# Weights loaded and split by whole blocks of 1024 columns, and q and k rotated by full-height products, in a float32 decoder step on one core

## The chip, the cores and the metric

The kernel runs on one core of one Trainium2 chip. The time is the device time of an execution in microseconds (us), and the number that counts is the median of several runs. Each core has a matrix engine (PE, with its weight loads shown apart as PEld), a vector engine (DVE), a scalar engine (ACT), a general engine (POOL) and a queue that starts the transfers (SP).

## The reference

The reference is one inference step of a hybrid decoder of two layers with 1024 features, all in float32. Two groups of requests share the weights: one prompt of 512 tokens and eight sequences of 4 new tokens each, so that 544 tokens go through every projection.

```python
for l in range(2):
    h = rms_norm(x, norm1_w[l])
    qr, kr, vr, gr, qa, ka, va = split(h @ w_in[l])         # 7 x 512 columns
    qr, kr = rotary(4 heads of 128), rotary(4 heads of 128)
    qa, ka = rotary(8 heads of 64), rotary(8 heads of 64)
    y = silu(gr) * group_norm(retention(qr, kr, vr, state_ret))
    o = dilated_attention(qa, ka, va, cache_k, cache_v)     # windows (128,1) (512,4) (2048,16)
    x = x + concat(y, o) @ w_out[l]
    x = x + (silu(g) * val) @ w_down[l]    # g, val: causal conv, width 3, of norm(x) @ w_up[l]
y = rms_norm(x, final_norm_w)

def rotary(x, pos):       # of one head, halves x1 and x2
    return concat([x1 * cos - x2 * sin, x2 * cos + x1 * sin])
```

Besides y it returns the rotated keys and the values of every new token, the retention states and the last rows that the convolution needs.

## The kernel before

**Layout.** Features lie on the partitions and tokens along a row: a tile of one block of 128 features is 128 x 544, and in PSUM two halves of 272 tokens (HC). The matrix engine multiplies in a reduced float32 form (fp32r), and the kernel gets float32 accuracy from three products: each weight and each activation is split into a high and a low part (wh and wl, xh and xl), and a block of 128 output features sums wh·xh, wh·xl and wl·xh over the blocks of the input. With 8 input blocks (nk = 8) that is 8 x 3 x 2 = 48 matmuls of 128 x 272; w_out (nk = 4, two passes of eight blocks) and w_down (nk 5, 5, 4, 4, 4 in five groups of eight blocks) have shorter blocks.

**The main list.** `main` holds all blocks in the order in which PE multiplies them: in each layer 28 blocks of w_in, 16 of w_out, 44 of w_up, 40 of w_down. In w_in the order is va0, va1, ka0, qa0, ka1, qa1, va2, ka2, qa2, va3, ka3, qa3, then vr, kr, qr for each of four heads, then the four gates; each of these blocks holds 128 columns, so a block of ka or qa holds two heads of 64 and a block of kr or qr one head of 128.

**Weights.** `add_block` cuts a block with nk over 4 in two parts of (nk+1)//2, so a w_in block comes in two parts of 512 columns; `halves` numbers the parts of all blocks with s. When PE's code comes to part s, `load_w(s+6)` puts the load of a later part on SP (tag raw, 6 buffers), and `split_w(s+3)` lets ACT copy part s+3 to wh and spawns DVE's subtraction that leaves wl (5 buffers each). PE's code for part s waits for that with `parts_of(s)`.

**Rotation.** Each block of q or k has an evacuation from PSUM (`ka(hp)`, `qa(hp)`, `kr(h)`, `qr(h)`) that calls `rotary_out`: DVE multiplies the whole block by cos (tile ra), and then, for each half of each head in it, the other half by sin (tile rb, pieces of 32 or 64 partitions); POOL adds the two, the 512 prompt tokens and the 32 sample tokens apart.

**What sets the order.** The code of the attention and the retention is written as generators, which `st.spawn` queues. While PE's code of the blocks is written out, `st.pump` and `st.until` step these generators, whenever a model of the engines' clocks (class Clock) says that their inputs are ready. So PE's blocks (tiles ps) are mixed with the attention's and the retention's small matmuls (tiles sec), and the place of each is fixed when the kernel is built. `blk` hands out 51 buffers in turn for all tiles of 128 x 544. Every instruction is recorded by one helper, so that nearly all of the trace's rows have line L112; they are told apart by their tiles.

Of the kernel before, what the change touches and what calls it, by code (L numbers as in the profile page):

```python
# [9 lines left out]
F32 = mybir.dt.float32  # L10
F32R = mybir.dt.float32r
# [6 lines left out]
NT = SEQ + NB * T  # L18
HC = NT // 2
PC = SEQ // 2  # L20
SC = NB * T // 2
KB = D // 128
ZB = 28
FB = 22
GROUPS = ((0, 5), (5, 10), (10, 14), (14, 18), (18, 22))
EPS = 1e-6
# [14 lines left out]
NPAR = 48  # L41
NCONV = 352
EARLY = 640


SEM = {"pe": 0.22, "act": 0.2, "dve": 0.14, "pool": 0.08, "sp": 0.1}
# [179 lines left out]
def trunk(ctx: ExitStack, tc: tile.TileContext, xin, w_in, w_out, w_up, w_down, kc, vc, s0, sctx_d, params_d,  # L226
# [69 lines left out]

    def add_block(src, nk, rhs, evac, pre=None):
        i = len(main)
        parts = [(0, nk)] if nk <= 4 else [(0, (nk + 1) // 2), ((nk + 1) // 2, nk)]
        main.append(dict(src=src, nk=nk, rhs=rhs, evac=evac, pre=pre, first=len(halves), parts=parts))  # L300
        for a, b in parts:
            halves.append((i, a, b))
# [3 lines left out]
    def load_w(s):  # L306
        if s < len(halves):
            i, a, b = halves[s]
            raw[s] = rotate(wpool.tile([128, b - a, 128], F32, name=name("raw"), tag="raw", bufs=6), "raw", 6)
            sp.dma_start(raw[s], main[i]["src"][:, a:b, :])  # L310

    def split_w(s, at_once=False):
        if s < len(halves):
            i, a, b = halves[s]
            if i >= len(main) - KB:
                hi, lo = (blk([128, b - a, 128], F32R, n) for n in ("wh", "wl"))
            else:
                hi, lo = (rotate(wpool.tile([128, b - a, 128], F32R, name=name(n), tag=n, bufs=5), n, 5)
                          for n in ("wh", "wl"))
# [160 lines left out]
    def two(ap, w):  # L480
        return ap.rearrange("p (c n) -> p c n", c=2)
# [2 lines left out]
        dve.tensor_mul(two(dst[:, 0:SEQ], PC), ps[:, :, 0:PC], rstd[:, :, 0:PC])  # L484
        dve.tensor_mul(two(dst[:, SEQ:NT], SC), ps[:, :, PC:HC], rstd[:, :, PC:HC])

    def rotary_out(ps, cos, sin, half, dst):
        a = blk([128, 2, HC], F32, "ra")
        b = blk([128, 2, HC], F32, "rb")
        dve.tensor_mul(a, ps[:, :, :HC], cos)  # L490
        for q in range(0, 128, 2 * half):
            lo, hi = slice(q, q + half), slice(q + half, q + 2 * half)
            dve.tensor_mul(b[lo], ps[hi, :, :HC], sin[hi])
            dve.tensor_mul(b[hi], ps[lo, :, :HC], sin[lo])
        pool.tensor_add(two(dst[:, 0:SEQ], PC), a[:, :, 0:PC], b[:, :, 0:PC])
        pool.tensor_add(two(dst[:, SEQ:NT], SC), a[:, :, PC:HC], b[:, :, PC:HC])

    def rsqrt_small(out, var, n):
        v = small([128, n], "rsv", 2)
# [382 lines left out]
    def mixer(l):  # L882
# [69 lines left out]
                store(kv_o[l, 1, hp], L.va[hp])  # L952
            return evac

        def ka(hp):
            def evac(ps):
                L.ka[hp] = blk([128, NT], F32, "ka")
                rotary_out(ps, *L.tab[2], 32, L.ka[hp])
                pool.tensor_copy(L.ks[:, hp, :], L.ka[hp][:, SEQ:])
                store(kv_o[l, 0, hp], L.ka[hp])  # L960
            return evac

        def qa(hp):
            def evac(ps):
                L.qa[hp] = blk([128, NT], F32, "qa")
                rotary_out(ps, *L.tab[2], 32, L.qa[hp])
                for s in range(2):
                    r = slice(64 * s, 64 * s + 64)
                    c = (2 * hp + s) * T
                    pool.tensor_copy(L.qpad[r, hp, :, c:c + T],  # L970
                                     L.qa[hp][r, SEQ:].rearrange("p (b t) -> p b t", b=NB))
                L.cat[4 + hp] = blk([128, 2, HC], F32, "cat")
                L.have.add(("qa", hp))
                if hp == 2:
                    start_ret()
                if hp == 3:
                    L.tab.pop(2)
                    rope_tables(L, l, 0)()
                    fold_tables(L, 0, norm)
            return evac  # L980

        def g(h):
            def evac(ps):
# [12 lines left out]
                scaled_out(ps, norm.rstd, L.vr[h])  # L996
            return evac

        def kr(h):
            def evac(ps):  # L1000
                L.kr[h] = blk([128, NT], F32, "kr")
                rotary_out(ps, *L.tab[0], 64, L.kr[h])
            return evac

        def qr(h):
            def evac(ps):
                L.qr[h] = blk([128, NT], F32, "qr")
                rotary_out(ps, *L.tab[0], 64, L.qr[h])
                L.cat[h] = blk([128, 2, HC], F32, "catr")
                L.have.add(("qr", h))  # L1010
                if h == 3:
                    L.tab.pop(0)
            return evac

        rhs = rhs_of(norm)
        order = [(24, va(0)), (25, va(1))]
        for hp in range(4):
            order += [(24 + hp, va(hp))] * (hp > 1) + [(20 + hp, ka(hp)), (16 + hp, qa(hp))]
        for h in range(4):
            order += [(8 + h, vr(h)), (4 + h, kr(h)), (h, qr(h))]  # L1020
        for h in range(4):
            order.append((12 + h, g(h)))
        for n, (zb, evac) in enumerate(order):
# [156 lines left out]
        else:  # L1180
            load_w(n)
    load_w(4)
    load_w(5)
    for what, n in start:
        if what == "x":
            list(first.scale(n))
# [19 lines left out]
    sp.dma_start(cst[0], consts_d[:, :EARLY])  # L1206
    ps = [main_bank() for _ in range(2)]
    for k in range(KB):
        if k == 4:
            load_w(6)  # L1210
            load_w(7)
            split_w(4)
        if k == 6:
            split_w(5)
            split_w(6)
        for n in range(2):
            s = 2 * n + k // 4
            products(main[n], ps[n], k, parts_of(s), k // 4 * 4)
            if k % 4 == 3:
                split.pop(s)  # L1220
            if k == KB - 1:
                main[n]["evac"](ps[n])
                ps[n] = None
            st.pump(0.7)
    load_w(8)
    load_w(9)
    sp.dma_start(cst[1], consts_d[:, EARLY:])
    sp.dma_start(taps, params_d[:, NPAR:])

    for i, b in enumerate(main[2:-KB]):  # L1230
        st.block = i + 2
        if b["pre"]:
            b["pre"]()
        ps = main_bank()
        for pi, (a, e) in enumerate(b["parts"]):
            s = b["first"] + pi
            load_w(s + 6)
            split_w(s + 3)
            w = parts_of(s)
            split.pop(s)  # L1240
            for k in range(a, e):
                products(b, ps, k, w, a)
                st.pump(0.7)
        b["evac"](ps)
        st.pump()
# [3 lines left out]
    for c in range(2):  # L1249
        for n, b in enumerate(main[-KB:]):  # L1250
            s, nk = b["first"], b["nk"]
            if c == 0:
                load_w(s + 6)
                split_w(s + 3)
# [14 lines left out]
def _tables():  # L1269
# [51 lines left out]
    for first, half in ((0, 64), (2, 32)):  # L1321
        e = (-np.arange(half, dtype=f) / f(half)).astype(f)
        inv = np.power(10000.0, e.astype(np.float64)).astype(f)
        ang = (p[None, :] * inv[:, None]).astype(f).astype(np.float64)
        cos, sin = _chunk(np.cos(ang).astype(f)), _chunk(np.sin(ang).astype(f))
        rope[:, first] = np.concatenate([cos] * (128 // half))
        rope[:, first + 1] = np.concatenate([sin, -sin] * (64 // half))
    return out, rope


# [6 lines left out]
def _layout(i):  # L1337
    g = {k: np.asarray(v) for k, v in i.items()}
    a = {}
    tok = np.concatenate([g["x_prompt"].reshape(SEQ, D), g["x_sample"].reshape(NB * T, D)])  # L1340
    a["xin"] = _chunk(tok.T.reshape(KB, 128, NT).transpose(1, 0, 2))

    def w(n):
        m = g[n]
# [50 lines left out]
```

## Time and profile before

| | |
|---|---|
| median of 3 runs | 1444.94 us (1444.93 to 1448.46) |
| profiled execution | 1444.82 us |
| its span | 1443.0 us |
| mean granted clock of PE | 0.997 |
| PE busy | 1423.1 us (99%) |
| DVE busy | 949.2 us (66%) |
| ACT busy | 571.6 us (40%) |
| POOL busy | 178.9 us (12%) |

The span is the time from the first to the last instruction of the profiled execution; 1.8 us of its own time lie around it. Busy is the sum of an engine's instructions; matmuls overlap one another, so PE at 99% says that it hardly ever lacked an instruction, and the time of one matmul is read from the spacing of starts.

### The profile page before, as it was taken

To read this page: it belongs to the slowest core of one execution; us is meant where nothing else is said; L and a number is where in the kernel's file an instruction comes from. 1 tells how busy PE (TensorE), PEld (TensorE's weight loads), DVE (VectorE), ACT (ScalarE), POOL (GpSimd) and SP (SyncE) were. 2 spreads that over 40 slices of the span, in tenths; PEclk is the share of its full clock that TensorE was granted. 3 is DMA by queue.
4 is the path that set the end of the run, shared out by engine and by line. 5 is a ranking of instruction groups with operands and counts; after the bars stand their busy time and mean duration, and the time that the engine had idled before them with its cause. 6 is when DMAs were issued, how large, how long until landed. Compare 5 with 4: busy or idle time off the path is not lost.

```text
span 1443.0 us, 29646 instructions
## 1 busy us (share of the span) xinstructions
PE 1423.1 (99%) x11634; PEld 1356.0 (94%) x11634; DVE 949.2 (66%) x1857; ACT 571.6 (40%) x1108; POOL 178.9 (12%) x553
## 2 busy tenths in 40 slices
PE   8999999999999999999999999999999999999997
PEld 8888788999999999999998878899999999999996
DVE  8876556588775565757678765566977647566665
ACT  4454333444443333424435442243444424333334
POOL 4212222000000000000022221120000000000003
PEclk9999999999999999999999999999999999999999
DMA  6315682433222222223322339722422232322231
GB/s 237 97 60 181 233 311 89 154 113 115 93 80 88 91 83 101 93 84 104 104 90 90 119 105 316 283 91 101 148 104 88 65 112 70 107 88 89 88 93 63
DMA packets 98635, 173.92 MB, mean 121 GB/s; under 512 B 11072, under 2 KB 21440, under 8 KB 98496
## 3 DMA queue, kind: packets, MB, share of 16 engines
q1 hardware_dynamic: 98496, 172.03, 35.3%
q8 instruction: 92, 1.51, 0.4%
q14 instruction: 47, 0.39, 0.1%
HBM read 159.77 MB, written 12.21 MB: 119 GB/s over the span
## 4 chain that ended last, share of the span: by engine, by line
PE 94%; DVE 3%; issue 1%; DMA 0%; ACT 0%; SPq 0%; DVEq 0%; POOL 0%; ACTq 0%
PE ps L112 82%; PE sec L112 12%; DVE wl L112 1%; DVE rb L112 1%; DMA x<-xin 0%; DVE p L112 0%; SPq L112 0%; DVE xl L112 0%; DVE ra L112 0%; DVE sq L112 0%; ACT xh L112 0%; DVE va L112 0%; POOL qa L112 0%; DVEq L1381 0%; DVE tmp L112 0%
## 5 line engine op out<-in xcount | busy, mean ns | idle before, releaser
L112 PE MATMUL ps<-xh,wh 128*128 128x272 f32 x2304 | 489.0, 294 | 1.4 <-ACT wh L112 1.1
L112 PE MATMUL ps<-xh,wl 128*128 128x272 f32 x2304 | 477.3, 289 | 0.7 <-DVE wl L112 0.7
L112 PE MATMUL ps<-xl,wh 128*128 128x272 f32 x2304 | 477.3, 289 | 0.0
L112 PEld LDWEIGHTS ps<-xh,wh 128*128 128x128 f32 x2304 | 361.2, 189 | 19.0 <-issue 14.7
L112 PEld LDWEIGHTS ps<-xh,wl 128*128 128x128 f32 x2304 | 362.3, 189 | 0.9 <-DVE wl L112 0.9
L112 PEld LDWEIGHTS ps<-xl,wh 128*128 128x128 f32 x2304 | 362.3, 189 | 0.0
L112 ACT ACTIVATE wh<-raw 128x512 fp32r<-128x512 f32 (+2 forms) x432 | 248.3, 598 | 172.0 <-PE ps L112 158.8
L112 DVE TENSOR_TENSOR wl<-raw,wh 128x512 fp32r<-128x512 f32 (+2 forms) x432 | 295.9, 703 | 18.7 <-ACT wh L112 17.9
L112 DVE SCALAR_TENSOR_TENSOR c<-u,taps,c 128x560 f32<-128x560 f32 x176 | 141.2, 802 | 89.0 <-ACT c L112 85.9
L112 ACT ACTIVATE c<-u,taps 128x560 f32<-128x560 f32 x88 | 75.5, 857 | 227.1 <-DVE u L112 223.7
L112 DVE TENSOR_TENSOR x<-x,ps 128x544 f32<-128x544 f32 (+1 forms) x120 | 81.7, 681 | 119.6 <-PE ps L112 119.2
L112 PE MATMUL ps<-yh,wh 128*128 128x272 f32 x704 | 150.9, 288 | 0.0
L112 PE MATMUL ps<-yh,wl 128*128 128x272 f32 x704 | 150.5, 288 | 0.0
L112 PE MATMUL ps<-yl,wh 128*128 128x272 f32 x704 | 150.4, 288 | 0.0
L112 DVE TENSOR_TENSOR u<-ps,rstd 128x512 f32<-128x512 f32 (+1 forms) x176 | 69.2, 435 | 80.5 <-PE ps L112 80.4
L112 PEld LDWEIGHTS ps<-yh,wh 128*128 128x128 f32 x704 | 112.3, 188 | 0.1
L112 PEld LDWEIGHTS ps<-yl,wh 128*128 128x128 f32 x704 | 112.2, 188 | 0.1
L112 PEld LDWEIGHTS ps<-yh,wl 128*128 128x128 f32 x704 | 112.3, 188 | 0.0
L112 POOL COPY last<-u 128x2 f32<-128x2 f32 (+1 forms) x176 | 28.2, 192 | 667.2 <-DVE u L112 630.3
L112 DVE TENSOR_TENSOR rb<-ps,rope 32x544 f32<-32x544 f32 (+1 forms) x96 | 69.2, 721 | 1.4
L112 ACT ACTIVATE yh<-y 128x544 fp32r<-128x544 f32 x44 | 29.0, 659 | 82.6 <-DVE y L112 82.6
L112 PE MATMUL ps<-ch,wh 128*128 128x272 f32 x256 | 53.4, 290 | 0.0
(147 smaller groups left out, 1343.3 us busy)
## 6 DMA issues: line engine op xcount, KB each, us to landing
raw<-w_up SPq DMA_DIRECT2D x176, 256.0 KB, 2.8
raw<-w_in SPq DMA_DIRECT2D x112, 256.0 KB, 3.9
kt<-kc SPq DMA_DIRECT2D x80, 256.0 KB, 5.2
vt<-vc SPq DMA_DIRECT2D x80, 256.0 KB, 5.2
raw<-w_down SPq DMA_DIRECT2D x48, 256.0 KB, 2.6
raw<-w_out SPq DMA_DIRECT2D x32, 256.0 KB, 2.7
raw<-w_down SPq DMA_DIRECT2D x32, 192.0 KB, 2.4
s<-s SPq DMA_DIRECT2D x16, 256.0 KB, 5.3
```

The lines of the kernel that those rows point to most:

```text
L112: return f(*args, **kw)
```

## The change

It has two parts. First, weights are loaded and split by whole blocks: only the first two blocks keep their two parts (their buffers come from `blk`), and for every other block there is one load, one copy to wh and one subtraction to wl, 128 x 1024 for nk = 8. There are 3 buffers each for raw, wh and wl in place of 6 and 5; the load of block s+3 stands at the start of block s, the split of block s+2 in its middle (in the last eight blocks at its start).

Second, the host reorders the columns of w_in for q and k, so that two neighbouring blocks (a pair g) hold the first halves and the second halves of the same heads: four heads of 64 or two of 128. `rotated` evacuates the first block by its products with cos and sin (both tiles named ra), the second likewise (rb), and POOL subtracts and adds them to r1 and r2, whose rows are still ordered by halves. Transfers then gather the halves of each head into the tiles qa, ka, qr, kr: eight of 32 x 544 for each pair of ka or qa, four of 64 x 544 for each pair of kr or qr, 96 in all. The copies for the sample tokens, the store of the keys and the note that a head is there (`L.have`) come behind the gather. The order of w_in is now va0, va1, ka0, ka1, qa0, qa1, va2, va3, ka2, ka3, qa2, qa3, then vr, vr, kr, kr, qr, qr twice, then the gates. The sign of the sine goes from the table to the subtraction.

```diff
 def add_block(src, nk, rhs, evac, pre=None):
     i = len(main)
-    parts = [(0, nk)] if nk <= 4 else [(0, (nk + 1) // 2), ((nk + 1) // 2, nk)]
+    parts = [(0, nk)] if i > 1 else [(0, nk // 2), (nk // 2, nk)]
...
 def load_w(s):
-        raw[s] = rotate(wpool.tile([128, b - a, 128], F32, name=name("raw"), tag="raw", bufs=6), "raw", 6)
+        if s < 4:
+            raw[s] = blk([128, b - a, 128], F32, "raw")
+        else:
+            raw[s] = rotate(wpool.tile([128, b - a, 128], F32, name=name("raw"), tag="raw", bufs=UNITS), "raw",
+                            UNITS)
...
-def rotary_out(ps, cos, sin, half, dst):
-    a = blk([128, 2, HC], F32, "ra")
-    b = blk([128, 2, HC], F32, "rb")
-    dve.tensor_mul(a, ps[:, :, :HC], cos)
-    for q in range(0, 128, 2 * half):
-        lo, hi = slice(q, q + half), slice(q + half, q + 2 * half)
-        dve.tensor_mul(b[lo], ps[hi, :, :HC], sin[hi])
-        dve.tensor_mul(b[hi], ps[lo, :, :HC], sin[lo])
-    pool.tensor_add(two(dst[:, 0:SEQ], PC), a[:, :, 0:PC], b[:, :, 0:PC])
-    pool.tensor_add(two(dst[:, SEQ:NT], SC), a[:, :, PC:HC], b[:, :, PC:HC])
+def rotated(tabs, half, dsts, after):
+    kept = []
+    def first(ps):
+        kept.extend(blk([128, 2, HC], F32, "ra") for _ in range(2))
+        for t, tab in zip(kept, tabs()):
+            dve.tensor_mul(t, ps[:, :, :HC], tab)
+    def second(ps):
+        bs = [blk([128, 2, HC], F32, "rb") for _ in range(2)]
+        for t, tab in zip(bs, tabs()):
+            dve.tensor_mul(t, ps[:, :, :HC], tab)
+        outs = [blk([128, NT], F32, n) for n in ("r1", "r2")]
+        for o, x0, x1, f in ((outs[0], kept[0], bs[1], pool.tensor_sub), (outs[1], bs[0], kept[1], pool.tensor_add)):
+            f(two(o[:, 0:SEQ], PC), x0[:, :, 0:PC], x1[:, :, 0:PC])
+            f(two(o[:, SEQ:NT], SC), x0[:, :, PC:HC], x1[:, :, PC:HC])
+        kept.clear()
+        tiles = dsts()
+        def gather(outs):
+            yield EW("sp", *outs)
+            per = 128 // (2 * half)
+            for i, d in enumerate(tiles):
+                for j in range(per):
+                    for n, o in enumerate(outs):
+                        q = 2 * half * j + half * n
+                        p = half * (i * per + j)
+                        sp.dma_start(d[q:q + half], o[p:p + half])
+            after(tiles)
+        st.spawn(gather(outs), "evac")
+    return first, second
...
-        load_w(s + 6)
-        split_w(s + 3)
+        load_w(s + 3)
         w = parts_of(s)
         for k in range(a, e):
+            if k == (a + e) // 2:
+                split_w(s + 2)
             products(b, ps, k, w, a)
```

Counted over the whole program, DVE has 1445 rows in place of 1619, ACT 848 in place of 1022, POOL 494 as before, and SP 606 transfers in place of 684. PE has the same matmuls; its code goes from a block to a run of sec matmuls and back 167 times, where it was 151.

On DVE, early in layer 0, this stood from the evacuation of ka0 (ps_333) to behind that of qa0 (ps_418); each part of a weight has its own wl.

```order
L112 TENSOR_TENSOR ra_408<-ps_333,rope_189 128x544
L112 TENSOR_TENSOR rb_409<-ps_333,rope_191 32x544 x4
L112 TENSOR_TENSOR wl_422<-raw_329,wh_421 128x512
L112 TENSOR_TENSOR wl_452<-raw_334,wh_451 128x512
L112 TENSOR_TENSOR ra_481<-ps_418,rope_189 128x544
L112 TENSOR_TENSOR rb_482<-ps_418,rope_191 32x544 x4
L112 TENSOR_TENSOR wl_507<-raw_367,wh_506 128x512
L112 TENSOR_TENSOR wl_537<-raw_419,wh_536 128x512
```

Now the same place holds the two blocks of ka (ps_323 and ps_395).

```order
L114 TENSOR_TENSOR ra_391<-ps_323,rope_187 128x544
L114 TENSOR_TENSOR ra_392<-ps_323,rope_189 128x544
L114 TENSOR_TENSOR wl_423<-raw_324,wh_422 128x1024
L114 TENSOR_TENSOR rb_450<-ps_395,rope_187 128x544
L114 TENSOR_TENSOR rb_451<-ps_395,rope_189 128x544
L114 TENSOR_TENSOR wl_490<-raw_396,wh_489 128x1024
```

Two blocks took ten products and four subtractions, and take four products and two subtractions of twice the columns.

On PE, the first scores of the attention (sec from ka and qa) stood behind 42 of the 48 matmuls of block 4, the block after qa0 was evacuated.

```order
L112 MATMUL ps_503<-xh_169,wh_421 128x272 x2
L112 MATMUL ps_503<-xl_171,wh_421 128x272 x2
L112 MATMUL ps_503<-xh_169,wl_422 128x272 x2
L112 MATMUL sec_558<-ka_407,qa_480 128x128
L112 MATMUL sec_560<-ka_407,qa_480 128x128
L112 MATMUL ps_503<-xh_173,wh_421 128x272 x2
```

Now they stand behind the first 6 matmuls of block 7, and qa is complete with block 5; block 6, in between, holds 48 matmuls and ten transposes of va.

```order
L114 MATMUL ps_698<-xh_116,wh_560 128x272 x2
L114 MATMUL ps_698<-xl_118,wh_560 128x272 x2
L114 MATMUL ps_698<-xh_116,wl_561 128x272 x2
L114 MATMUL sec_708<-ka_460,qa_598 128x128
L114 MATMUL sec_710<-ka_460,qa_598 128x128
L114 MATMUL ps_698<-xh_126,wh_560 128x272 x2
L114 MATMUL ps_698<-xl_128,wh_560 128x272 x2
L114 MATMUL ps_698<-xh_126,wl_561 128x272 x2
L114 MATMUL sec_728<-ka_461,qa_599 128x128
L114 MATMUL sec_730<-ka_461,qa_599 128x128
```

The distance from the end of qa's block to the scores was 42 matmuls and is now 54 and the ten transposes.

On SP, between two loads of weights there was at most one other transfer here, such as the store of a key tile.

```order
L112 DMA raw_449<-w_in 128x512
L112 DMA kv_o<-ka_407 128x544
L112 DMA raw_504<-w_in 128x512
L112 DMA raw_534<-w_in 128x512
L112 DMA raw_590<-w_in 128x512
```

Now the eight transfers that gather the two tiles of qa stand between two loads.

```order
L114 DMA raw_607<-w_in 128x1024
L114 DMA qa_598<-r_89_592 32x544
L114 DMA qa_598<-r_90_593 32x544
L114 DMA qa_598<-r_89_592 32x544
L114 DMA qa_598<-r_90_593 32x544
L114 DMA qa_599<-r_89_592 32x544
L114 DMA qa_599<-r_90_593 32x544
L114 DMA qa_599<-r_89_592 32x544
L114 DMA qa_599<-r_90_593 32x544
L114 DMA raw_699<-w_in 128x1024
```

What stands behind them on SP, the next load first, is issued after them.

## Rows read from the trace of the kernel before

**Rows 1.** The page's head: the span, and each engine's busy time, share and instructions.

```profile
span 1443.0 us, 29646 instructions
PE 1423.1 (99%) x11634; PEld 1356.0 (94%) x11634; DVE 949.2 (66%) x1857; ACT 571.6 (40%) x1108; POOL 178.9 (12%) x553
```

**Rows 2.** Three windows: length, busy time by engine, granted clock, transfer share, GB/s.

```profile
20.00:50.00 30.00, 28.66 (x223) 27.73 (x222) 28.86 (x44) 8.38 (x19) 10.01 (x10) 1.00 0.37 130
300.00:335.00 35.00, 35.00 (x272) 34.53 (x271) 33.04 (x54) 17.31 (x29) 0.70 (x5) 1.00 0.41 138
335.00:500.00 165.00, 165.00 (x1319) 165.00 (x1318) 108.88 (x194) 66.71 (x109) 11.43 (x92) 1.00 0.28 93
```

**Rows 3.** The chain that ended last: share of the span by engine.

```profile
PE 94%; DVE 3%; issue 1%; DMA 0%; ACT 0%; SPq 0%; DVEq 0%; POOL 0%; ACTq 0%
```

**Rows 4.** PE's waits: whom it waited for, us in total, times, the longest.

```profile
PE sec L112 <- DVE p L112: 5.0, 4, 1.8
...
PE ps L112 <- DVE wl L112: 0.7, 1, 0.7
...
PE sec L112 <- POOL qa L112: 0.5, 1, 0.5
```

**Rows 5.** Groups of instructions by shape: busy time, mean ns, idle before.

```profile
L112 DVE TENSOR_TENSOR wl<-raw,wh 128x512 fp32r<-128x512 f32 x368 | 267.2, 740 | 18.7 <-ACT wh L112 17.9
L112 ACT ACTIVATE wh<-raw 128x512 fp32r<-128x512 f32 x368 | 220.5, 621 | 127.6 <-PE ps L112 118.3 <-issue 6.8 <-DMA raw<-w_down 1.2
L112 DVE TENSOR_TENSOR rb<-ps,rope 32x544 f32<-32x544 f32 x64 | 46.1, 720 | 0.9
L112 DVE TENSOR_TENSOR ra<-ps,rope 128x544 f32<-128x544 f32 x32 | 23.1, 722 | 28.4 <-PE ps L112 28.3
L112 DVE TENSOR_TENSOR rb<-ps,rope 64x544 f32<-64x544 f32 x32 | 23.1, 722 | 0.5
L112 DVE TENSOR_TENSOR wl<-raw,wh 128x256 fp32r<-128x256 f32 x32 | 13.4, 419 | 0.0
L112 ACT ACTIVATE wh<-raw 128x256 fp32r<-128x256 f32 x32 | 13.1, 411 | 27.6 <-PE ps L112 27.6
```

**Rows 6.** PE's timeline at two places in layer 0: start, length, instruction.

```profile
52.59 0.40 PE L112 MATMUL ps<-xh,wl 128*128 128x272 f32 x2
52.92 0.44 PE L112 MATMUL sec<-pt,vt 128*64 128x128 f32 x4
...
53.64 0.41 PE L112 MATMUL ps<-xl,wh 128*128 128x272 f32 x2
...
115.42 0.41 PE L112 MATMUL ps<-xh,wl 128*128 128x272 f32 x2
115.76 1.09 PE L112 MATMUL sec<-pt,vt 128*64 128x128 f32 x16
...
117.14 0.41 PE L112 MATMUL ps<-xl,wh 128*128 128x272 f32 x2
```

**Rows 7.** Timeline of DVE and POOL at three places in layer 0.

```profile
41.16 2.38 DVE L112 TENSOR_TENSOR wl<-raw,wh 128x512 fp32r<-128x512 f32 x2
...
41.21 2.44 POOL L112 TENSOR_TENSOR qa<-ra,rb 128x512 f32<-128x512 f32 x2 [3.39 <-DVE rb L112]
...
176.96 1.50 POOL L112 TENSOR_TENSOR qr<-ra,rb 128x512 f32<-128x512 f32 x2 [5.86 <-PE sec L112]
...
302.20 0.68 DVE L112 TENSOR_TENSOR wl<-raw,wh 128x512 fp32r<-128x512 f32 x1
```

**Rows 8.** Transfers by kind: KB each, and median us from issue to landing.

```profile
raw<-w_in SPq DMA_DIRECT2D x112, 256.0 KB, 3.9
...
kv_o<-ka SPq DMA_DIRECT2D x8, 272.0 KB, 2.1
...
pret_o<-ss SPq DMA_DIRECT2D x8, 64.0 KB, 1.5
```

**Rows 9.** SP's timeline near 51 us: start, length and number of issues.

```profile
51.50 1.36 SPq L112 DMA_DIRECT2D raw<-w_in  x3
```

More of the change, by code (lines that the diff above doesn't have):

```diff
@@ L23 @@
 ZB = 28
+D_IN = ZB * 128
 FB = 22
@@ L43 @@
 EARLY = 640
+UNITS = 3
 SEM = {"pe": 0.22, "act": 0.2, "dve": 0.14, "pool": 0.08, "sp": 0.1}
@@ L314, in split_w @@
             i, a, b = halves[s]
-            if i >= len(main) - KB:
+            if s < 4 or i >= len(main) - KB:
                 hi, lo = (blk([128, b - a, 128], F32R, n) for n in ("wh", "wl"))
             else:
-                hi, lo = (rotate(wpool.tile([128, b - a, 128], F32R, name=name(n), tag=n, bufs=5), n, 5)
+                hi, lo = (rotate(wpool.tile([128, b - a, 128], F32R, name=name(n), tag=n, bufs=UNITS), n, UNITS)
                           for n in ("wh", "wl"))
@@ L953, in va, with ka, tiles, after @@
             return evac
[L955 to L974, printed above, removed]
+        def ka(g):
+            def tiles():
+                return [blk([128, NT], F32, "ka") for _ in range(2)]
+            def after(t):
+                for hp, k in zip((2 * g, 2 * g + 1), t):
+                    L.ka[hp] = k
+                    pool.tensor_copy(L.ks[:, hp, :], k[:, SEQ:])
+                    store(kv_o[l, 0, hp], k)
+            return rotated(lambda: L.tab[2], 32, tiles, after)
+        def qa(g):
+            def tiles():
+                return [blk([128, NT], F32, "qa") for _ in range(2)]
+            def after(t):
+                for hp, q in zip((2 * g, 2 * g + 1), t):
+                    L.qa[hp] = q
+                    for s in range(2):
+                        r = slice(64 * s, 64 * s + 64)
+                        c = (2 * hp + s) * T
+                        pool.tensor_copy(L.qpad[r, hp, :, c:c + T], q[r, SEQ:].rearrange("p (b t) -> p b t", b=NB))
+                    L.cat[4 + hp] = blk([128, 2, HC], F32, "cat")
+                    L.have.add(("qa", hp))
+            first, second = rotated(lambda: L.tab[2], 32, tiles, after)
+            def last(ps):
+                second(ps)
+                if g == 0:
                     start_ret()
-                if hp == 3:
+                else:
                     L.tab.pop(2)
@@ L979, in evac @@
                     fold_tables(L, 0, norm)
-            return evac
+            return first, last
         def g(h):
@@ L997, in vr, with kr, tiles, after @@
             return evac
[L999 to L1011, printed above, removed]
+        def kr(g):
+            def tiles():
+                return [blk([128, NT], F32, "kr") for _ in range(2)]
+            def after(t):
+                L.kr[2 * g:2 * g + 2] = t
+            return rotated(lambda: L.tab[0], 64, tiles, after)
+        def qr(g):
+            def tiles():
+                return [blk([128, NT], F32, "qr") for _ in range(2)]
+            def after(t):
+                for h, q in zip((2 * g, 2 * g + 1), t):
+                    L.qr[h] = q
+                    L.cat[h] = blk([128, 2, HC], F32, "catr")
+                    L.have.add(("qr", h))
+            first, second = rotated(lambda: L.tab[0], 64, tiles, after)
+            def last(ps):
+                second(ps)
+                if g == 1:
                     L.tab.pop(0)
-            return evac
+            return first, last
         rhs = rhs_of(norm)
[L1016 to L1020, printed above, removed]
+        order = []
+        for i in range(2):
+            order += [(24 + 2 * i, va(2 * i)), (25 + 2 * i, va(2 * i + 1))]
+            order += [*zip((20 + 2 * i, 21 + 2 * i), ka(i)), *zip((16 + 2 * i, 17 + 2 * i), qa(i))]
+        for i in range(2):
+            order += [(8 + 2 * i, vr(2 * i)), (9 + 2 * i, vr(2 * i + 1))]
+            order += [*zip((4 + 2 * i, 5 + 2 * i), kr(i)), *zip((2 * i, 2 * i + 1), qr(i))]
         for h in range(4):
@@ L1182, in trunk @@
     load_w(4)
-    load_w(5)
     for what, n in start:
@@ L1208, in trunk @@
     for k in range(KB):
+        if k == 2:
+            load_w(5)
         if k == 4:
+            split_w(4)
             load_w(6)
-            load_w(7)
-            split_w(4)
         if k == 6:
             split_w(5)
-            split_w(6)
         for n in range(2):
@@ L1224, in trunk @@
             st.pump(0.7)
-    load_w(8)
-    load_w(9)
     sp.dma_start(cst[1], consts_d[:, EARLY:])
@@ L1252, in trunk @@
             if c == 0:
-                load_w(s + 6)
-                split_w(s + 3)
+                load_w(s + 3)
+                split_w(s + 2)
             ps = main_bank()
@@ L1326, in _tables @@
         rope[:, first] = np.concatenate([cos] * (128 // half))
-        rope[:, first + 1] = np.concatenate([sin, -sin] * (64 // half))
+        rope[:, first + 1] = np.concatenate([sin] * (128 // half))
     return out, rope
@@ L1341, in _layout @@
     a["xin"] = _chunk(tok.T.reshape(KB, 128, NT).transpose(1, 0, 2))
+    z = np.arange(D_IN)
+    for at, heads, half in ((0, 2, 64), (512, 2, 64), (2048, 4, 32), (2560, 4, 32)):
+        z[at:at + 512] = z[at:at + 512].reshape(2, heads, 2, half).transpose(0, 2, 1, 3).reshape(-1)
+    g["w_in"] = g["w_in"][:, :, z]
     def w(n):
```

## The prediction

> **What bounds the kernel now.** I read the page's head first. PE is busy for 1423.1 us of a span of 1443.0 us, so whatever the change does to the other engines, it can win at most the 19.9 us between them, the start and the end of the program included [rows 1]. The chain that ended last says the same from the other side: 94% of it is PE, 3% DVE, 1% issue [rows 3]. Next the windows. In the 165 us of a stretch of the feed-forward part, PE is never idle, and 1319 matmuls take 165.00 us: 0.125 us each, at the full clock (1.00, the level of 2.4 GHz) [rows 2]. There DVE has 108.88 us of work in 165, ACT 66.71, and nothing that makes them faster is seen by PE. In the attention's stretch from 20 to 50 us it is otherwise: DVE is busy for 28.86 us of 30 and PE for only 28.66, and in w_out from 300 to 335 us DVE is busy for 33.04 of 35 while PE still loses nothing [rows 2]. Last I read whom PE waits for in the middle of the kernel: four waits for DVE's softmax tile p are 5.0 us, one for a wl 0.7, one for POOL's qa 0.5, in sum 6.2 us [rows 4]. This is what a lighter DVE and POOL can give back. All else is PE's own work, and the change leaves the matmuls as they are.
>
> **The change part by part.**
>
> *Rotation.* Before, 32 products ra, 64 pieces rb of 32 partitions and 32 of 64 partitions take 23.1 + 46.1 + 23.1 = 92.3 us, each of them 0.720 to 0.722 us, whatever its height [rows 5]. That a full-height product costs no more than a piece is seen here, so 64 of them take 64 × 0.722 = 46.2 us: DVE loses 46 us of work. POOL keeps its number of operations.
>
> *Splits.* 174 fewer of them: 142 blocks with nk = 8 and 32 with nk = 5. The trace has no 128 x 1024, so I extend the two sizes that it has. From 256 to 512 columns wl grows from 0.419 to 0.740 us on the mean [rows 5], or to 0.68 undisturbed [rows 7]; two more such steps give 1.20 to 1.38, against 1.36 to 1.48 for two of 512. A merged split thus saves 0.10 to 0.16 us on DVE, 17 to 28 us in all. On ACT the steps are 0.411 and 0.621 us [rows 5], so 1.04 for one in place of 1.24, and 35 us in all.
>
> *What this is worth.* DVE loses 63 to 74 of its 949 us, but all of it beside PE. In the feed-forward part PE covers it wholly. In the mixers it is worth at most the 6.2 us of waits; it is worth nothing if those are waits of a chain (scores, softmax, transposes) whose length does not hang on DVE's queue. Since DVE is nearly full exactly where they stand, the value is nearer the upper end: I take −5 us, and keep 0 to −6.2.
>
> *The first whole split.* The block behind the two divided ones now needs a wl of 1.20 us in place of one of 0.68 near the start, where nothing is prepared ahead: +0.5 us (0 to 0.5).
>
> *More switches of PE.* PE goes 16 times more from a block to sec matmuls and back. Around four records of pt,vt, from the start of the row ahead to the one behind it (52.59 to 53.64), 1.05 us pass, of which the four block matmuls between these starts take 0.50, so 0.55 are left; around sixteen records it is 117.14 − 115.42 = 1.72, less 0.50, so 1.22 [rows 6]. Twelve more records cost 0.67 us, 0.056 each, which leaves a fixed 0.33 us for a run. This is the upper price of a switch; the lower is 0, if that part belongs to the first matmul of a new tile and not to the switch. I take the middle, 0.15: 16 × 0.15 = +2.4 us (0 to 5.3).
>
> *The gather.* This is a new wait, and the one that I fear most. From the end of qa's second block: two products on DVE, 1.44 us [rows 5]; then POOL's r1 and r2. A pair of its operations (512 and 32 tokens) takes 1.50 us undisturbed and 2.44 beside DVE's wl, which is itself slower there, two of them in 2.38 us [rows 7]; two pairs take 3.0 to 4.9. Then the transfers: the first of a tile's four needs only r1, so three more issues come behind r2, each 1.36 / 3 = 0.45 us [rows 9], that is 1.4. A transfer of the gather has 68 KB; the nearest rows land 1.5 us (64 KB) and 2.1 us (272 KB) after issue, while weights take 3.9 [rows 8]. I take 1.5 to 2.1, since these two also start in SBUF. The chain is 1.44 + 3.0 + 1.4 + 1.5 = 7.3 us at the least and 1.44 + 4.9 + 1.4 + 2.1 = 9.8 at the most. PE gets to the first scores after 54 block matmuls and ten transposes, which at 0.125 us are 8.0 us. So PE waits 0 to 1.8 us, and where it does, the second tile, four issues (1.8 us) later, adds up to 0.8, since PE arrives there only eight matmuls (1.0 us) later. Two pairs of qa in each of two layers give four such places: 0 to 10.4 us. I take 1.0 us each, +4 us, a little under the middle, as DVE is lighter than in these rows and so disturbs POOL less. For qr the retention comes later in its block, and I put nothing there.
>
> Against the gather stands a rule of the Trainium skill, page "SBUF — State Buffer", section "The DMA setup-cost knee": every transfer pays about 2 us, however small it is. The 64 KB row, 1.5 us from issue to landing, is below that, so the measurement decides; by the page's figures (2 us, and 68 KB at 436 GB/s) a landing would be an estimate of 2.2 us, the chain's least 8.0, and the term nearer +6 than +4.
>
> *SP and the weights' lead.* The gather's eight issues take 3.6 us, and behind them wait the next load and all that SP holds; they also wait for POOL. Loads are put on SP three blocks ahead, 18 us at 48 × 0.125 = 6 us a block, and land in 3.9 [rows 8]; the lateness of 3.6 + 4.9 is inside that, so it costs nothing. Were that cover gone, each microsecond would be PE's, at eight gathers a layer. The splits have a lead of one and a half blocks in place of three parts: 9 us where blocks take 6, and 4.5 us in w_out and w_down, where they take 3. ACT's copy 0.62 and DVE's wl 0.74 fit in, with 3 us to spare for what else DVE holds; nothing again.
>
> Sum: −5 + 0.5 + 2.4 + 4 = +1.9 us on the profiled 1444.8 us, 1446.7, say 1447. The profiled execution and the median of the runs shown differ by 0.1 us.
>
> **The rivals.** *DVE's relief counts in full (faster).* DVE at 28.86 of 30 us beside PE's waits for p speaks for it [rows 2, 4]. If all 6.2 us come back, the gathers end at the short end of their chain, and a switch costs 0.05: −6.2 + 0.5 + 0.8 = −4.9, about 1440. Against it: the term needs every wait to vanish and no new one to appear.
>
> *The gather is late (slower).* If POOL's pairs stay at 2.44 us, as in the only row beside a split, each of the four places costs 2.6 us; with waits for p of which then only 3 us come back, −3 + 0.5 + 2.4 + 10.4 = +10.3, about 1455. It decides from 9.8 − 8.0 = 1.8 us of lateness on; a chain under 8.0 us costs nothing. The other pieces for PE (the caches' attention) can't fill in, as PE takes its code in order.
>
> *The short lead of splits (slower).* In w_out DVE is busy for 33.04 of 35 us [rows 2], and a product or a softmax piece in front of wl takes 0.7 us; five of these in a row exceed the 3 us to spare. 16 blocks in each layer at 0.25 us are 8 us, and with the sum's 1.9 about 1455. Against it: PE loses nothing there now, and DVE gets no more work there.
>
> *The change makes DVE no lighter:* the equal 0.72 us of ra and both sizes of rb speaks against it [rows 5], and I give it no share.
>
> **How the numbers follow.** About 0.3%, 4.3 us, is what can be told from no change here. The sum stays within that, 1441 to 1449, as long as its terms move by less than 6 us down or 2.5 up: chance 0.45. The full relief has 0.27, the late gather 0.19, the short lead 0.09. Hence faster 0.27, same 0.45, slower 0.28. The range goes from under the faster rival to the two slower ones, 1438 to 1455; above it lies a gather at its worst together with switches at 0.33, with no relief: 0.5 + 5.3 + 10.4 = 16.2, or 1461.
>
> **What would show it.** In the changed kernel's profile: DVE's busy time near 880 us; 64 products ra and rb of about 0.72 us; a wl of 128 x 1024 of 1.2 to 1.4. PE's waits should have less on p, and a new row, sec waiting for a transfer qa<-r, of some 4 us; a row over 8 us there means the late gather, none at all the faster rival. A wait of ps for wl in w_out means the short lead. PE's busy time tells the switches: about 2 us more. The prediction is wrong if PE's blocks themselves run at another pace, or if SP's queue holds back a raw load until PE waits for it.

## The result and the profile after

The changed kernel takes 1453.91 us (median of 6 runs, 1452.12 to 1459.02) where the kernel before takes 1445.06 (6 runs): a ratio of 1.0061, interval [1.0042, 1.0080]. It is slower by 8.9 us. The kernel before itself takes 1444.7 to 1445.5 us in some executions, at a mean granted clock of 0.995 to 0.998, and up to 1448.8 in others, at 0.993 to 0.994, so its median moves by 1.5 us with the share of each. The forecast of 1447 called "no change" the likeliest; the time lies inside the range, near the 1455 of the case called "the gather is late".

The page's head of the changed kernel, in the columns of [rows 1]:

```profile
span 1454.2 us, 28810 instructions
PE 1433.2 (99%) x11634; PEld 1364.6 (94%) x11634; DVE 876.7 (60%) x1619; ACT 554.7 (38%) x934; POOL 173.0 (12%) x553
```

DVE has lost 72.5 us of work, as planned, and the span has grown by 11.2 us in this execution (1456.21 us). The three windows of [rows 2] say the same stage by stage:

```profile
20.00:50.00 30.00, 29.66 (x233) 29.31 (x232) 19.70 (x26) 6.20 (x8) 7.41 (x8) 1.00 0.37 115
300.00:335.00 35.00, 35.00 (x275) 34.74 (x274) 31.17 (x48) 19.09 (x27) 0.30 (x2) 1.00 0.44 151
335.00:500.00 165.00, 165.00 (x1313) 164.76 (x1312) 110.36 (x168) 62.97 (x78) 13.00 (x88) 1.00 0.29 94
```

From 20 to 50 us DVE is busy for 19.70 us in place of 28.86, and PE does 233 matmuls in place of 223. In the feed-forward stretch PE is busy all the time in both. The groups of instructions that answer to [rows 5], by shape:

```profile
L114 DVE TENSOR_TENSOR wl<-raw,wh 128x1024 fp32r<-128x1024 f32 x142 | 176.9, 1246 | 51.9 <-ACT wh L114 49.7
...
L114 DVE TENSOR_TENSOR rb<-ps,rope 128x544 f32<-128x544 f32 x32 | 21.7, 719 | 57.6 <-PE ps L114 57.6
L114 DVE TENSOR_TENSOR ra<-ps,rope 128x544 f32<-128x544 f32 x32 | 21.6, 718 | 23.3 <-PE ps L114 23.3
```

What PE waits for, in the columns of [rows 4]:

```profile
PE sec L114 <- DMA qa<-r: 3.5, 5, 0.9
PE sec L114 <- issue: 1.8, 3, 0.7
PE sec L114 <- DVE p L114: 1.5, 4, 0.4
```

The wait for p has shrunk from 5.0 to 1.5 us, and the new wait for the gather has taken its place, 3.5 us and most of the 1.8 put down to issue (these stand before the same scores). Waits alone thus balance. What they set off does not balance, as the first of the four places shows. SP's timeline there (start, length, number of issues):

```profile
52.56 6.75 SPq L114 DMA_DIRECT2D qa<-r  x8
59.41 0.53 SPq L114 DMA_DIRECT2D raw<-w_in  x1
```

PE's timeline at the same place, block matmuls left out:

```profile
57.35 0.49 PE L114 MATMUL sec<-ka,qa 64*128 64x128 f32 x2
58.38 0.46 PE L114 MATMUL sec<-ka,qa 64*128 64x128 f32 x2 [0.55 <-issue]
...
59.73 0.48 PE L114 MATMUL sec<-ka,qa 64*128 64x128 f32 x2
60.88 0.76 PE L114 MATMUL sec<-ka,qa 64*128 64x128 f32 x2 [0.66 <-DMA qa<-r]
```

And windows of 2 us from there on, with the columns of [rows 2]:

```profile
58.00:60.00 2.00, 1.62 (x10) 1.38 (x10) 1.06 (x8) 0.99 (x4) 0.41 (x2) 1.00 0.46 111
60.00:62.00 2.00, 1.34 (x6) 0.95 (x6) 0.85 (x6) 0.49 (x2) 0.21 (x1) 0.61 0.86 188
62.00:64.00 2.00, 2.00 (x11) 2.00 (x11) 0.34 (x2) 0.46 (x2) 0.00 (x0) 0.50 0.93 336
64.00:66.00 2.00, 2.00 (x10) 2.00 (x10) 0.45 (x2) 1.08 (x4) 0.00 (x0) 0.50 0.41 168
66.00:68.00 2.00, 2.00 (x13) 1.71 (x12) 1.23 (x1) 0.62 (x2) 0.00 (x0) 0.68 0.00 0
```

SP issues the last of eight transfers at the end of 6.75 us, it lands at 60.7, and PE, which stood twice, each time before a tile's second head, has done 10 and 6 matmuls in two windows; in `filled`, below, the same windows hold 18 each. Within the second wait, at about 60.5, the granted clock falls to 0.50, which is 1.2 GHz, and it stays there until about 67.3, though PE is busy again from 60.9: 11 and 10 matmuls in the next two windows.

### The profile page after: what moved, and what is told of

It is laid out like the page before. It is cut to its first block, busy times and chain, and to the rows that moved or that the text cites. A ratio compares the mean times of both kernels' runs of the same rounds, so it can differ in the third digit from the quotient of the medians.

```text
span 1454.2 us, 28810 instructions
## 1 busy us (share of the span) xinstructions
PE 1433.2 (99%) x11634; PEld 1364.6 (94%) x11634; DVE 876.7 (60%) x1619; ACT 554.7 (38%) x934; POOL 173.0 (12%) x553
## 4 chain that ended last, share of the span: by engine, by line
PE 93%; DVE 3%; DMA 1%; SPq 1%; POOL 1%; issue 0%; ACT 0%; DVEq 0%; ACTq 0%; POOLq 0%
PE ps L114 82%; PE sec L114 11%; DVE p L114 2%; SPq L114 1%; DMA qa<-r 1%; POOL r L114 1%; DVE rb L114 1%; DMA x<-xin 0%; DVE ra L114 0%; DVE wl L114 0%; DVE tmp L114 0%; DVE pm L114 0%; DVE va L114 0%; DVEq L1435 0%; DVE yo L114 0%
## 5 line engine op out<-in xcount | busy, mean ns | idle before, releaser
L114 ACT ACTIVATE wh<-raw 128x1024 fp32r<-128x1024 f32 (+2 forms) x258 | 225.0, 873 | 238.9 <-PE ps L114 191.6
L114 DVE TENSOR_TENSOR wl<-raw,wh 128x1024 fp32r<-128x1024 f32 (+2 forms) x258 | 262.4, 1018 | 52.4 <-ACT wh L114 50.2
L114 POOL COPY last<-u 128x2 f32<-128x2 f32 (+1 forms) x176 | 32.3, 216 | 659.3 <-DVE u L114 659.3
L114 POOL TENSOR_TENSOR r<-ra,rb 128x512 f32<-128x512 f32 (+1 forms) x32 | 29.5, 942 | 296.2 <-DVE pm L114 139.3
L114 DVE CUSTOM_DVE_ANT_0 p<-sec,cst 128x128 f32<-128x128 f32 (+3 forms) x64 | 30.1, 489 | 46.7 <-PE sec L114 45.5
```

What stands on the lines that cost most here:

```text
L114: return f(*args, **kw)
```

## The experiments

The theory, **A**: the loss is the late gather, by PE's waits for it and the slower clock behind them. Rival **B**: the order of PE's code, with 16 more switches. Rival **C**: the weights by whole blocks. All kernels below were timed in five rounds against the kernel before on their chip (median there 1446.5 us).

**One part of the change alone, and no gather.** `weights_only` is the kernel before with the change's hunks on loads and splits; `rotation_only` the kernel before with those on the rotation. In `no_gather`:

```diff
-                            sp.dma_start(d[q:q + half], o[p:p + half])
+                            sp.charge("dma_start", [d[:half]], [o[:half]], (), {})
```

with the tiles r1 and r2 given on in place of d, and their due time in the planner set to d's.

> The kernel before with the weights' part of the change alone (whole blocks, 3 buffers), rotation as before. Theory A, the late gather: all of the loss comes with the rotation, so this is 1443 to 1446 us, at most 0.7 us above before for the first whole split, and no window after 20 us shows a granted clock under 1. Rival B, the switches (152 runs of sec matmuls here become 156): about +1 us. Rival C, the whole blocks themselves: 1450 us or more, with waits of ps for wl or wh.

> The kernel before with the rotation by full-height products and gathers alone, weights in parts as before. Theory A: 1450 to 1456 us, waits of sec for qa<-r of some 3 to 6 us, and stretches of lower granted clock behind them. Rival B (164 runs of sec in place of 152): about 1449, without any lower clock. Rival C: 1443 to 1446.

> The changed kernel without its 96 gather transfers: scores, stores and the retention read r1 and r2 in their order by halves, so which rows belong to which head is left out; every row on PE, DVE, ACT and POOL stands in the same order as in the changed kernel. Theory A: the waits for qa<-r (3.5 us, and 1.8 us put down to issue) and the slower clock behind them vanish: 1444 to 1448 us. Rival B, switches and order, which are the same here: 1451 us or more. Rival C, the whole blocks: 1451 or more.

| kernel | median us | ratio, interval | PE busy |
|---|---|---|---|
| before | 1446.5 | | 1423.1 |
| weights_only | 1448.41 | 1.0013 [1.0005, 1.0022] | 1423.8 |
| rotation_only | 1458.83 | 1.0087 [1.0073, 1.0101] | 1432.5 |
| no_gather | 1441.47 | 0.9965 [0.9953, 0.9977] | 1422.3 |

Without 96 transfers, and with every row of the computing engines in its place, 12.4 us vanish (1453.9 to 1441.5), and the rest of the change is a gain of 5. The profiled executions of before and of `no_gather`, whose mean granted clock is 0.997 in both, differ by 3.3 us only. The range of `no_gather` was missed downwards: the gather cost more than its waits. That of `rotation_only`, 1450 to 1456, was missed upwards. It waits for qa<-r as expected, but the waits for p are still there, although DVE has 57 us less to do than before (892.4 us):

```profile
PE sec L113 <- DVE p L113: 6.3, 4, 1.6
PE sec L113 <- DMA qa<-r: 4.4, 7, 0.9
```

B falls in this form: the 168 runs of sec matmuls are still there, and PE's busy time is 0.8 us under that of before. C falls as the main cause: the whole blocks alone cost 1.9 us by the medians and 3.7 between the profiled executions, both more than the 0.7 expected. PE's waits in that kernel:

```profile
PE sec L113 <- DVE p L113: 6.8, 8, 1.1
PE ps L113 <- DVE wl L113: 1.4, 1, 1.4
PE sec L113 <- DVE pm L113: 1.3, 4, 0.4
```

And a stretch of DVE's timeline in it:

```profile
45.29 0.72 DVE L113 TENSOR_TENSOR ra<-ps,rope 128x544 f32<-128x544 f32 x1
46.02 2.92 DVE L113 TENSOR_TENSOR rb<-ps,rope 32x544 f32<-32x544 f32 x4
48.97 0.17 DVE L113 RECIPROCAL pm<-pm 128x1 f32<-128x1 f32 x1
49.17 1.26 DVE L113 TENSOR_SCALAR p<-p,pm 128x128 f32<-128x128 f32 x1
50.36 1.28 DVE L113 TENSOR_TENSOR wl<-raw,wh 128x1024 fp32r<-128x1024 f32 x1
```

The old rotation, which this kernel keeps, holds DVE for 3.6 us, the softmax's small operations come behind it and around the larger splits, and PE waits for p: 6.8 us in place of 5.0. The scaling of p there (TENSOR_SCALAR, by the reciprocal of the softmax's sum) takes 1.26 us for 128 columns, where one such takes 0.29 in the changed kernel's mean; it runs beside an addition of POOL's:

```profile
49.09 1.48 POOL L113 TENSOR_TENSOR ka<-ra,rb 128x512 f32<-128x512 f32 x2 [4.92 <-DVE rb L113]
```

Scalings of p that take over 0.8 us all run beside an operation of POOL's; the kernel before has 8 of them and this one 16. `sums_dve`, below, takes POOL's additions away and has none of them. Where each loss falls is seen by comparing when PE starts a block, around the four places (blocks counted over the whole program, times in us from the timelines):

| from the start of block to the next | no_gather | changed | r1_first | filled | true_cost |
|---|---|---|---|---|---|
| 7 to 8 | 9.99 | 14.93 | 12.07 | 12.19 | 8.58 |
| 13 to 14 | 9.97 | 13.94 | 12.05 | 12.84 | 8.57 |
| 135 to 136 | 9.98 | 13.68 | 13.59 | 12.19 | 8.56 |
| 141 to 142 | 9.94 | 12.09 | 15.06 | 12.18 | 8.74 |

The changed kernel loses 4.9, 4.0, 3.7 and 2.2 us at the four places, in sum 14.8 in this execution; that is the whole of the 14.7 us between its profiled execution (1456.21) and that of `no_gather` (1441.52). At the last place the granted clock stays at 1.00, so 2.2 us is what the waits cost there; the clock fell at the other three, where up to 2.8 more are lost. The column of `true_cost` is no loss or gain by itself: in its plan other sec matmuls stand in these blocks (18 records in place of 28).

**The transfers in another order.** `r1_first` has the loop over r1 and r2 outermost.

```diff
-                for i, d in enumerate(tiles):
-                    for j in range(per):
-                        for n, o in enumerate(outs):
+                for n, o in enumerate(outs):
+                    for i, d in enumerate(tiles):
+                        for j in range(per):
```

> The changed kernel with each pair's transfers issued with all pieces of r1 ahead of all pieces of r2, so that four of eight go while POOL still makes r2. Theory A: the last piece is issued some 2 us earlier (6 issues of 0.59 us behind r2 in the place of 7 become 4), the second tile's wait of about 0.9 us vanishes at its four places, the first tile's stays; with less of the slower clock 1448 to 1452 us. Rivals B and C: no change from the changed kernel, 1452 to 1456.

1453.25 us, 1.0054 [1.0036, 1.0073]: no gain that can be told. The expectation of A was wrong in its detail: at two places the cost is 2.1 us, hardly under the 2.2 of before. PE's waits in its profile explain it: it now waits at each of the four heads' scores, 0.73, 0.19, 0.19 and 0.16 us in the first place, and short waits between pieces cost what two longer ones did. At the other two places the clock fell. The planner's order changed a little with it, too (164 runs of sec matmuls in place of 168).

**Work in place of the wait.** `filled` puts matmuls on constants before the first scores, in the same order else.

```diff
             t = sec([128, 512])
+            if i == 0 and s == 0:
+                for _ in range(FILL):    # 5
+                    nc.tensor.matmul(t[:, :128], lhsT=ones, rhs=ones, start=True, stop=True)
             pe.matmul(t[:, :n], ...
```

> The changed kernel, every row in its order, with five more matmuls of 128 x 128 on constants (about 1.1 us) on PE ahead of the first scores of each pair of heads, 40 in all, so that PE works through most of the 1.7 us for which it waited at each of four places. Theory A1, the waits cost their length and, where the granted clock falls behind them, that too: the clock stays at 1.00 from 20 us on, the waits for qa<-r nearly vanish, and the time is that without the gather, 1441.5, plus 8 x 1.1 = 8.8, about 1450, below the changed kernel's 1453.9 although PE has more to do. Rival A2, the slower clock has nothing to do with the waits: it still shows, and the time is 1454 or more.

```profile
58.00:60.00 2.00, 2.00 (x18) 1.88 (x19) 1.19 (x8) 0.88 (x4) 0.20 (x1) 1.00 0.45 107
60.00:62.00 2.00, 2.00 (x18) 1.76 (x18) 0.88 (x7) 0.56 (x3) 0.21 (x1) 1.00 0.83 254
62.00:64.00 2.00, 2.00 (x19) 2.00 (x18) 0.67 (x3) 1.78 (x6) 0.00 (x0) 1.00 0.98 394
```

In the profile the point is clear: no wait for qa<-r, no slower clock at any place (the windows beside those of the changed kernel above), and the four places take 9.5 us over no_gather with the fill, against 14.8 with the waits. That the slower clock comes with such waits is thus shown; it does not come with each of them, as the fourth place of the changed kernel has them at 1.00. But the time forecast from it was wrong: 1455.54 us (1453.67 to 1456.32), not 1450, so the fill is no gain over the changed kernel. The profiled execution is the fastest, and 12.1 us over no_gather, of which the places are 9.5. Of the other 2.6, 2.5 lie in four blocks behind the places (17, 23, 145 and 146), in two of which PE waits for a load of the caches (kt<-kc, 0.8 us), a wait that neither the changed kernel nor no_gather has; why the other executions take up to 2.6 us more stays open.

**The gather on time.** `true_cost` changes one number: the planner takes SP's time for a gather transfer as measured.

```diff
                             sp.dma_start(d[q:q + half], o[p:p + half])
+                            clock.now["sp"] += 0.53
```

`sums_dve` lets DVE do the subtraction and the addition; `all_three` has both and r1's transfers first.

> The changed kernel with the planner charging SP 0.59 us for each gather transfer, as measured, in place of 0.06; this moves the first scores 12 matmuls (1.5 us) later and the second tile's 24 (3 us) later in their block, and other pieces with them. Theory A: waits for qa<-r vanish and with them the slower clock, 1441 to 1445 us. Rival B, order and switches: no gain, 1450 or more.

> The changed kernel with r1 and r2 made by DVE (0.7 us for 512 tokens) in place of POOL (1.5 to 2.4); the planner puts the first scores 12 matmuls (1.5 us) earlier. The chain from qa's second block to the gather's end gets some 2.4 us shorter. Theory A: each of the four places loses some 0.9 us of its wait, 1447 to 1451 us. Rival B, or DVE's queue being the limit: 1453 or more, with longer waits for p.

> Sums on DVE, r1's pieces issued first and the planner charging 0.59 us a transfer, together. Theory A: no wait for qa<-r is left, the clock stays full behind 20 us, and the time is that of the kernel without the gather or a little above, 1441 to 1444 us, which would be under the kernel before. Rival B: 1448 or more.

`true_cost` takes 1435.32 us, 0.9922 [0.9909, 0.9935]: 18.6 us under the changed kernel, 11 under the kernel before and 6 under its expectation. All of PE's waits in its profile:

```profile
PE sec L114 <- DVE eps L114: 1.1, 1, 1.1
PE ps L114 <- ACT wh L114: 1.0, 1, 1.0
PE ps L114 <- DVE wl L114: 1.0, 1, 1.0
PE ps L114 <- DVE va L114: 0.3, 1, 0.3
```

All but the last are in the first 25 us. The gather is as slow as before (eight issues in 6.76 us), but PE has other work until it has landed. The waits for p (1.7 us in no_gather) are gone too; in all PE waits 3.4 us in place of 7.2. That is 3.8 of the 6.2 us by which it beats no_gather; in the rest PE is busy for 2.4 us less, and why is open. `sums_dve` gains nothing: 1453.63 us, 1.0055 [1.0041, 1.0070], with 3.8 us of waits for qa<-r and 2.0 for issue, but none for p; the planner spent the shorter chain by putting the scores 12 matmuls earlier. `all_three`, 1452.14 us, 1.0042 [1.0029, 1.0055], failed its expectation by 8 us: the waits for qa<-r are gone, but another gather is late. PE's timeline in layer 0:

```profile
166.95 0.42 PE L114 MATMUL ps<-xh,wl 128*128 128x272 f32 x2
170.72 1.62 PE L114 MATMUL sec<-qr,kr 128*128 128x128 f32 x6 [3.35 <-DMA qr<-r]
```

And SP's, ahead of it:

```profile
158.00 2.80 SPq L114 DMA_DIRECT2D kt<-kc  x5
160.90 2.11 SPq L114 DMA_DIRECT2D vt<-vc  x4
163.26 2.40 SPq L114 DMA_DIRECT2D qr<-r  x4
```

PE waits 9.3 us in three waits for qr. Four transfers of 136 KB stand behind nine of the caches' 256 KB, and land 6.1 us after issue at this place.

**Which edit moves the wait to qr, and is there a price for switches?** Four more: `cost_double` charges 1.06 in place of 0.53; `rotation_true` adds the charge to `rotation_only`; `r1_true` is r1 first with the charge; `sums_true` sums on DVE with the charge.

> As the kernel with the planner's charge of 0.59 us for each gather transfer (1435.3 us), but with 1.12 us: the first scores stand 12 matmuls later again, and PE has 166 runs of sec matmuls in place of 154. Theory A, lateness alone: the gather is as far from PE as before or farther, no wait for qa<-r, 1434 to 1437 us. Rival B, a price of 0.17 to 0.33 us for each switch, which a part of the gain of the 0.59 us kernel over the one without the gather (154 runs against 168, 6 us) would then be: 12 more runs are 2 to 4 us, 1437 to 1440.

> The rotation part alone (weights in parts as before) with the planner's charge of 0.59 us for each gather transfer. If the whole blocks are worth something once DVE is relieved (they saved 5 us between the rotation alone, 1458.8, and the whole change, 1453.9), this is slower than the 1435.3 us with both, 1437 to 1441; if their effect is that of their own run alone (+2 us), it is 1432 to 1435. Either way PE has no waits for qa<-r.

> The planner's charge of 0.59 us with r1's transfers issued first; sums on POOL. If the waits for qr<-r of 9.3 us in the kernel with all three edits came from the sums on DVE (which let the planner put the retention's scores earlier), they are not here, and the time is 1434 to 1437; if from the order of the transfers, they are here, and it is 1440 or more.

> The planner's charge of 0.59 us with the sums on DVE; transfers in the change's order. If the sums on DVE brought the waits for qr<-r, they are here, some 9 us, and the time is 1444 us or more; if the order of the transfers did, they are not, and it is 1434 to 1438.

| kernel | median us | ratio, interval | landing of qr<-r, median us | PE's wait for qa, qr, us |
|---|---|---|---|---|
| true_cost | 1435.32 | 0.9922 [0.9909, 0.9935] | 2.3 | 0, 0 |
| cost_double | 1437.33 | 0.9935 [0.9922, 0.9948] | 6.3 | 0, 0 |
| r1_true | 1442.10 | 0.9971 [0.9962, 0.9981] | 3.8 | 0, 2.6 |
| sums_true | 1442.86 | 0.9974 [0.9965, 0.9983] | 3.5 | 1.9, 1.0 |
| rotation_true | 1451.14 | 1.0032 [1.0019, 1.0045] | 5.9 | 0, 7.3 |

`cost_double` has 12 runs of sec matmuls more than `true_cost` and is 2.0 us slower, at the border of what the two theories gave. Its PE waits 2.2 us once for a wl, but in the first 25 us, where every execution differs a little:

```profile
PE ps L114 <- DVE wl L114: 3.1, 2, 2.2
```

From the start of block 2 to that of the last block both wait for 0.3 us only and the clock stays at 1.00, and `cost_double` takes 1396.4 us where `true_cost` takes 1394.6. So up to 0.16 us are left for each of the 12 runs; as the order differs in other ways too, the exact price of a switch stays open. `rotation_true` is far from either expectation: not the size of the blocks of weights was tried by it, but the place that qr's gather happens to get; so what whole blocks are worth beside the new rotation was not isolated. And neither single cause for qr's lateness holds (the time of `sums_true` lies in neither of its two ranges): qr lands late in four of the five, with either edit and with neither, and whether PE waits depends on where its scores stand (in `cost_double` they are late enough for 6.3 us). The planner does not know the landing behind other transfers.

## Why the prediction came out as it did

**The relief was right in size, but its cause was not as told.** Predicted 63 to 74 us off DVE and −5 us of time; measured 72.5 us, and with the gather taken out −5 by the medians and −3.3 between the profiled executions, the switches and the first split included. The wait for p fell from 5.0 to 1.5 us. But that it fell because DVE is lighter is not shown: with either part of the change alone DVE is lighter too (by 57 and 18 us), and the waits for p are 6.3 and 6.8 us. They follow operations of DVE that run beside POOL and take longer there. Two of the four waits before are of 1.7 to 1.8 us, behind scalings of p like this one, and two of 0.8, behind splits beside POOL's additions (a pair of 2.40 us, a single one of 1.78):

```profile
144.18 1.96 POOL L112 TENSOR_TENSOR qr<-ra,rb 128x512 f32<-128x512 f32 x2 [7.45 <-DVE rb L112]
146.10 1.26 POOL L112 TENSOR_TENSOR qd<-qr,cst 128x512 f32<-128x512 f32 x1
146.13 1.50 DVE L112 TENSOR_SCALAR p<-p,pm 128x512 f32<-128x512 f32 x1
...
147.69 1.36 PE L112 MATMUL sec<-cst,p 128*128 128x128 f32 x8 [1.75 <-DVE p L112]
```

In `true_cost` no scaling is beside POOL, all sixteen of 512 columns take about 0.49 us, and PE never waits for p:

```profile
91.54 0.49 DVE L114 TENSOR_SCALAR p<-p,pm 128x512 f32<-128x512 f32 x1
```

The changed kernel has four long ones of 1.32 us, one ahead of each of its four waits for p. The three kernels that let DVE make the sums have none, and no wait for p, although DVE is busy for 17 to 19 us more in them than in the changed kernel. That points to POOL's additions beside the scalings and not to DVE's load, though it is not proved: the plan differs in these kernels, too, and `cost_double` has four long scalings for which PE does not wait, as it comes to them later. Why the scalings are longer there, no run shows. Of the 6.2 us that the prediction counted in the middle of the kernel, the 0.7 for a wl lie in the first 25 us; 0.7 us for ACT's pt, which it did not count, lie in the middle. A merged split saves more than estimated: 1.246 us against 2 × 0.740.

**The step that failed is the gather's term, +4 us.** It measures +12.4 us, 2 us above the upper bound of 10.4. Its chain was right in kind. In the part that can be read at the first place, POOL's two pairs take 3.95 us (in the range 3.0 to 4.9) and a transfer lands in 2.0 us (1.5 to 2.1). But an issue of a gather transfer takes 0.59 to 0.62 us, not the 0.45 read from loads of weights [rows 9], and a pair of tiles needs seven behind r2: SP's queue ends 4.3 us behind r2. So each place costs 2.2 us where 1.0 was taken (2.6 was the bound), 8.6 for four at that price. The remaining 3.8 us were not in the sum at all: in the profile the places that cost more than 2.2 us are those with the granted clock at 0.50 in the waits and behind them, and the prediction priced waits by their length alone. How much of the 3.8 is the clock's can't be told closely: of the six executions the slowest takes 1459.0 us at a mean clock of 0.989, but one at 0.997, the clock of no_gather, still takes 1452.1, which is 10.6 over it, so some 2 us beside the 8.6 are not accounted for there.

That 1453.9 comes near the late gather's 1455 is in part luck. Its condition was POOL at 2.44 us a pair, where the first place has one of 1.5 and one of 2.5, and its sign, over 8 us of waits for qa<-r, did not come: the row has 3.5, with the issue waits 5.3, close to the 4 of the main case. It was right because it priced a place at 2.6 us, near the 2.2 measured, and because a slower clock that it did not know of and its other terms (−0.1 in sum, measured −3.3 to −5) went opposite ways.

The page "SBUF — State Buffer" of the Trainium skill, section "The DMA setup-cost knee", gives about 2 us for any small transfer; the gather's median of 2.0 for 68 KB agrees with it, better than the 64 KB row of before (1.5). By that rule the term would have been +6, still half of what was measured.

**The switches, +2.4 us, did not show:** with the same 168 runs and no gather, PE's busy time is 1422.3 us, under 1423.1. That does not make a switch free, as the order differs in other ways too: the 0.15 us taken is about what `cost_double` leaves at most for one. **The first whole split, +0.5 us, can't be told from the scatter:** PE's block 2 starts at 24.69 us in the changed kernel, at 23.99 before and at 24.27 in no_gather, but over all kernels here it is 24.04 to 24.89 with whole blocks and 23.99 to 24.43 with parts. **The splits' shorter lead cost next to nothing** in w_out: from the start of block 28 to that of block 44 it is 52.2 us in the changed kernel and 52.0 before, in layer 1 52.3 and 51.8, and PE waits for no wl there. SP's queue held back no load that PE waited for.

## What to carry to other kernels

Work taken off an engine beside the bound pays only by the waits that it ends, and a transfer put into a chain must be charged issue by issue, with what it has ahead of it in its queue. Where the order is planned from a model of the engines, a new kind of operation needs its measured cost there before its worth can be judged: one number, 0.59 us in place of 0.06, turned 8.9 us of loss into some 10 us of gain. An engine that is lighter need not give back a wait: look at what stands beside the operation that is waited for. A gain or a loss measured on one plan can belong to the plan; move the plan once, and look again.

## What the runs showed of the hardware

An issue on SP of a transfer of 32 x 544 took 0.59 us and more in a row, against 0.45 of a load of weights. Landing was slower with traffic ahead: 2.3 to 2.4 us for 136 KB in the changed kernel's medians, 6.1 behind nine loads of 256 KB. DVE's scaling of 128 x 512 took 0.49 us alone and up to 1.5 beside POOL's additions. And short waits can cost more than they last: where PE had stood for 0.55 us and stood again for 0.66, its granted clock was 0.50 (1.2 GHz) from about 60.5 to 67.3 us, though it was busy again from 60.9; where constants' matmuls filled these waits, it stayed at 1.00 (2.4 GHz).
